# Spilling mix chunks from the used gate tile by another queue, and tying a weight's squares and parts to matmuls of the group before

## The chip, the core and the metric

The kernel runs on one core of a Trainium2 chip. A core has five engines that run their own instruction streams in order and meet only at semaphores: TensorE (matmul, "PE" in the profile, its weight loads "PEld"), VectorE ("DVE"), ScalarE ("ACT"), GpSimd ("POOL") and SyncE ("SP"), which here only issues DMAs. Matmuls write to PSUM, other operands lie in SBUF. The metric is the device time of one launch in microseconds; less is better.

## The reference

Two layers of a hybrid decoder, 512 tokens, model width 2048, float32. Cut to what matters:

```python
def _layer(x, ...):
    h = _rmsnorm(x, norm_g)
    proj = h @ w_in                       # 2048 x 7696
    (cv_h, cv_b, cv_c, cv_g, sb_q, sb_k, sb_v, sb_g,
     gl_q, gl_k, gl_v, gl_g, gl_lr) = jnp.split(proj, split_points, axis=-1)
    y_conv = _short_conv(cv_h, cv_b, cv_c, conv_w, conv_b) * silu(cv_g)
    y_sb = _stick_breaking(rms(sb_q), rms(sb_k), sb_v) * silu(sb_g)       # 8 heads of 128
    g = log_sigmoid(gl_lr @ gla_w_up + gla_b_up) / 16
    y_gla = _rmsnorm(_gla(gl_q, gl_k, gl_v, g), gla_on_g) * silu(gl_g)     # 4 heads, dk 64, dv 128
    mix = jnp.concatenate([y_conv, y_sb, y_gla], axis=-1)
    return x + mix @ w_out                # 2048 x 2048
```

`y_conv = B * conv3(C * h)` is a causal convolution of width 3. Stick-breaking attention weighs key j of query i by `sigmoid(z_ij)` times the product of `sigmoid(-z_ik)` over the keys k between them. `_gla` is gated linear attention with a decay per key channel. The gate of every branch is `silu` of its own projection.

## The kernel before

**Precision and groups.** Every large product is made of float16 parts: an operand is split into a high part and a low rest, and a product takes three matmuls (high by high, high by low, low by high). The weight columns of a layer are cut into 38 groups of 256 (30 of `w_in`, 8 of `w_out`; the list `specs`, lines 318 to 334), worked off one after the other. The order in a layer is: GLA v 0, v 1, q, k, gate 0, gate 1; conv h, c, g, b of half 0; then for j = 0 to 3 attention v, g, q, k; conv h, c, g, b of half 1; then the eight output groups. The text calls them "v 0", "g 0" (the gate of attention pair 0), "conv b" and so on.

**One weight's way.** `fetch(i)` (350) loads weight i as two halves of 1 MB into one of two staging buffers "st", from GpSimd's queue (SyncE's for the first three). `wmax` (366) has ScalarE square each half into a junk tile and add up, which gives two sums per partition; these are "the squares" (line 370). `wscale` (376) adds them over partitions on GpSimd (383) and makes a power of two of it on VectorE (386 to 400). `whi` and `wlo` (433, 442) write the parts: ScalarE the high part (436), VectorE the rest (444), a half at a time, into the pools "wh" and "wl" of three buffers each. When the last part is written the staging buffer is free, and the fetch of the weight after the next may start.

**Quick groups.** `QUICK_IN` and `QUICK` name groups (all attention g and k, conv h 1, some output groups) that are multiplied by a Strassen-like scheme with seven block products instead of eight (`project_quick`, 735; matmuls on lines 750 and 753). Their weight is split by `wsums` (462) into seven blocks, with sums of blocks between; one of these sums is made by an accumulating DMA from GpSimd (494). The parts take all three buffers of the pools and an extra pair, "w7". The sums of the activations that they need are made once per layer by `xsums` (727) for the input groups and `msums` (717) for the output groups.

**Where products land.** Three PSUM banks ("psp") serve all groups; each group takes two. In `project_quick` the accumulators pa and pd share one bank, pb and pf the other; pa and pd are copied or added to the output tile on lines 761 to 775, and a product into a bank waits for the copy that reads the same bank.

**Order of the work.** The order on each engine is not written by hand (except for the prologue, lines 107 to 645): a planner sets it when the kernel is built, from a priority (order in the program; `tc.high_priority` lifts it), readiness on a modelled clock, and free buffers. Tiles of one tag get their buffers in program order. `order(a, b)` (190) and `tc.issue_after` add an edge of issue order for the planner; they put no semaphore into the program. `weights()` (506) is called at the head of each group i: it fetches weight i + 2 and calls `load(i + 1)` (339, 449), which places squares, scale and parts of the next weight at high priority; the squares come behind `anchor[i]`, the first high part of weight i (the third or second of a quick one).

**The mix.** The outputs of the branches ("chunks" of 128 channels, 16 a layer) become two float16 parts in `mixsplit` (847): ScalarE the high one (857), VectorE the rest (858). Until the tile for all chunks exists, the parts of a chunk go into a "ga" buffer of the work pool, and SyncE spills them to DRAM (860, 256 KB each, 12 a layer); `mixload` (862) brings them back later. The work pool has two buffers per tag. "ga" is also the scratch tile of the gates in `project_gate` (802): for GLA and conv gates the chain is line 822 (copy out of PSUM), 824 to 826 and 828 on ScalarE, 827 and 829 on VectorE. The gates themselves lie in "g" tiles, two buffers: GLA gate 0, GLA gate 1, the conv gate, then g 0, g 1 and so on. A gate is last read where a branch output is multiplied by it: lines 1109 (GLA), 1161 (conv), 1247 (attention). Conv b's accumulators are read on line 1176, which needs the product of 1161.

**The tail of the GLA.** The loop at 999 handles two pairs of heads. At its end stand, per head, 1096 (VectorE), 1098 (ScalarE), 1100 (a matmul that averages squares), 1102 and 1103 (ScalarE), 1104 to 1109 (VectorE), then `mixsplit`. `conv_out` (1158) follows it in the program, then the attention loop (1254).

Of the kernel before, what the change touches and what calls it, by code (L numbers as in the profile page):

```python
# [17 lines left out]
P = 128  # L18
# [25 lines left out]
def hybrid_trunk(ctx, tc, x, norm_g, w_in, conv_w, conv_b, sb_qn_g, sb_kn_g,  # L44
# [294 lines left out]
    def load(i):  # L339
        with tc.high_priority():  # L340
            load_(i)

# [23 lines left out]
    def wmax(i, h):  # L366

        if h == 0:
            peak[i] = sm(2 + (i in narrow), "wm")
        S.activation(junk(HK * GW).rearrange("p (k n) -> p k n", k=HK), staged[i][h], AF.Square,  # L370
                     accum_out=peak[i][:, h:h + 1])
        if h and i in narrow:
            S.activation(junk(KT * LR).rearrange("p (k n) -> p k n", k=KT), narrow[i], AF.Square,
                         accum_out=peak[i][:, 2:3])

    def wscale(i):

        l, src, cols = specs[i]

        m = sm(1, "wq")  # L380
        if i:
            gm = sm(2 + (i in narrow), "wgm")
            G.partition_all_reduce(gm, peak.pop(i), P, RED.add)  # L383
            if i in narrow:
                V.tensor_tensor(gm[:, 0:1], gm[:, 0:1], gm[:, 2:3], ALU.add)
            V.tensor_tensor(m, gm[:, 0:1], gm[:, 1:2], ALU.add)
        else:

            ps = bank(psm, "m")[:, :1]
            pk = peak.pop(i)  # L390
            for j, (a, b) in enumerate(((ones, pk[:, 0:1]), (ones, pk[:, 1:2]), (pk[:, 2:3], pk[:, 2:3]))):
# [12 lines left out]

# [26 lines left out]
    anchor = {}  # L431

    def whi(i, h):
        wh = wpool.tile([P, HK, GX], F16, tag="wh", name=nm("wh"))
        wl = wpool.tile([P, HK, GX], F16, tag="wl", name=nm("wl"))
        hi = S.activation(wh[:, :, :GW], staged[i][h], AF.Copy, scale=scales[i])  # L436
        anchor.setdefault(i, hi)
# [23 lines left out]

    def wsums(i):
# [18 lines left out]
        if specs[i][1] is w_out:  # L481
# [6 lines left out]
            anchor[i] = split(b12, 2)  # L488
# [7 lines left out]
        anchor[i] = split(b22, 3)  # L496
# [9 lines left out]
    def weights():  # L506
# [3 lines left out]
        if i + 2 < len(specs):  # L510
            with tc.high_priority():
                fetch(i + 2)
        if i and i + 1 < len(specs):
            load(i + 1)
# [132 lines left out]
    for l in range(depth):  # L647
# [3 lines left out]
        def project_cols():  # L651
# [3 lines left out]
            for h in range(2):  # L655
                wh, wl = w[h]
                for c, o in enumerate(ps):
                    cs = slice(c * P, (c + 1) * P)
                    for kk in range(HK):
# [5 lines left out]
                        T.matmul(o, wl[:, kk, cs], xh[:, :, k, :], start=False, stop=en)  # L665
            return ps, u

        def tok_mm(o, ah, al, w, t, k, n, st_, en):
# [4 lines left out]
            T.matmul(o, al[:, t, k, :], wh[:, kk, :n], start=False, stop=en, skip_group_check=True)  # L673

        def project_toks(ah, al, late=()):
# [59 lines left out]
        def project_quick(src, sums, y, cols):  # L735
# [7 lines left out]
            def prod(o, w, a, start, stop=False):  # L743
                for t in range(1 if cols else 2):
                    for kk in range(HK):
                        for i, (p_, q_) in enumerate(((0, 0), (0, 1), (1, 0))):
                            st_ = start and t == kk == i == 0
                            en = stop and kk == HK - 1 and i == 2
                            if cols:
                                T.matmul(o, w[q_][:, kk, :], a[p_][:, :, kk, :], start=st_, stop=en,  # L750
                                         skip_group_check=True)
                            else:
                                T.matmul(o[:, t * P:(t + 1) * P], a[p_][:, t, kk, :], w[q_][:, kk, :], start=st_,  # L753
                                         stop=en, skip_group_check=True)
# [7 lines left out]
            prod(pb, wT2, s_, True)  # L762
# [26 lines left out]
        def project_by_token(ah, al, n):  # L789
# [3 lines left out]
            for t in range(NT):  # L793
                o = bank(psp, "p")
                for i, (a_, part) in enumerate(((ah, 0), (al, 0), (ah, 1))):
                    for k in range(KT):
                        T.matmul(o[:, :n], a_[:, t, k, :], w[k // HK][part][:, k % HK, :n],  # L797
                                 start=i == 0 and k == 0, stop=i == 2 and k == KT - 1)
# [48 lines left out]
        def mixsplit(k, y, s_):  # L847
# [6 lines left out]
            else:  # L854
                hl = wk([P, 2, NT, P], "ga", dt=F16)
# [3 lines left out]
            if not mix:  # L859
                nc.sync.dma_start(mixd[l][:, :, k, :], hl.rearrange("p i t c -> p (i t) c"))  # L860
# [74 lines left out]
        insums = xsums()  # L935
# [10 lines left out]
        for tag in ("qT", "kT"):  # L946
# [17 lines left out]
            qku.append(un)  # L964
        gq, gk = qk
# [33 lines left out]
        for p in range(2):  # L999
# [92 lines left out]
            for hh in range(2):  # L1092
# [17 lines left out]
                mixsplit(12 + 2 * p + hh, o_, gsc[p])  # L1110
# [47 lines left out]
        def conv_out(j, y, then=lambda: None):  # L1158
# [20 lines left out]
            for c in range(2):  # L1179
                mixsplit(2 * j + c, y[:, c, :], s_)  # L1180
# [10 lines left out]
        def attend(j, qT, kT, vh, vl, vu, g, s_):  # L1191
# [34 lines left out]
            def values(hh):  # L1226
# [23 lines left out]
                mixsplit(4 + 2 * j + hh, y.rearrange("p t c -> p (t c)"), s_)  # L1250
# [157 lines left out]
```

## Time and profile before

| | us |
|---|---|
| median of 3 runs | 1780.85 (1779.24 to 1786.48) |
| profiled execution | 1789.68 |
| its span | 1787.5 |
| TensorE busy | 1685.7 |
| VectorE busy | 1340.1 |
| ScalarE busy | 1131.2 |
| GpSimd busy | 218.2 |
| mean granted clock of TensorE | 0.981 |

The profile is of one execution. In its rows "L370" is line 370 of the kernel; "junk<-st" names the tiles written and read. A row of the timeline has start, duration, engine, line, operation, tiles and shape, and in brackets how long the engine stood idle just before it and what ended that. A row of the waits has who waited for whom: microseconds in total, times, the longest. Where several semaphores were waited for, the last one is named.

### The profile page before, as it was taken

How to read it: one execution, taken by the hardware profiler on the slowest of the kernel's cores; microseconds unless marked ns; L12 is line 12 of the kernel's file. 1: busy time of each engine (PE TensorE's matmuls, PEld its weight loads, DVE VectorE, ACT ScalarE, POOL GpSimd, SP SyncE). 2: the span in 40 equal slices, each digit the busy share in tenths (PEclk: the TensorE clock that was granted, in tenths of full speed). 3: DMA queues.
4: the chain of work that ended last, by engine and by line, in shares of the span. 5: the costliest groups of instructions: out<-in, count | busy, mean ns of one | idle time of the engine just before them, and what ended most of it. 6: DMA issues, size and time to landing. Idle time of an engine off the chain costs nothing.

```text
span 1787.5 us, 36869 instructions
## 1 busy us (share of the span) xinstructions
PE 1685.7 (94%) x15642; PEld 1306.6 (73%) x15642; DVE 1340.1 (75%) x2327; ACT 1131.2 (63%) x1619; POOL 218.2 (12%) x262
## 2 busy tenths in 40 slices
PE   7999995999999999999989999959999899999999
PEld 5644554888989884689976454649888888748898
DVE  8966887577777787686688577866777777768874
ACT  7667664576666676566665675556676666755652
POOL 1210110011111111011111101001111111100100
PEclk9999998999999999999999999989999999999999
DMA  7233341357656867355544233224576677763441
GB/s 241 92 98 95 95 118 55 76 131 136 143 136 143 143 166 206 77 163 169 192 98 142 90 100 106 60 59 111 110 170 103 138 134 165 223 150 102 158 144 49
DMA packets 204517, 227.25 MB, mean 127 GB/s; under 512 B 118770, under 2 KB 166204, under 8 KB 203840
## 3 DMA queue, kind: packets, MB, share of 16 engines
q0 software_dynamic: 58432, 162.54, 32.6%
q1 hardware_dynamic: 136912, 52.90, 14.4%
q10 hardware_dynamic: 9008, 9.45, 1.6%
q8 instruction: 122, 2.00, 0.5%
q14 instruction: 43, 0.35, 0.1%
HBM read 179.65 MB, written 14.68 MB: 109 GB/s over the span
## 4 chain that ended last, share of the span: by engine, by line
PE 19%; DVE 13%; DMA 12%; ACT 7%; issue 3%; POOL 1%; POOLq 0%; ACTq 0%; DVEq 0%
DMA st<-in_w_in_dram 5%; PE psp L753 5%; ACT junk L370 3%; DMA st<-in_w_out_dram 3%; PE psp L797 3%; DVE wl L477 3%; DMA qT<-qp 2%; PE psp L673 2%; PE psp L750 2%; PE psp L671 2%; PE psp L672 2%; PE psp L664 1%; PE psp L663 1%; PE psp L665 1%; DVE wl L444 1%
## 5 line engine op out<-in xcount | busy, mean ns | idle before, releaser
L370 ACT ACTIVATE junk<-st 128x2048 uint8<-128x2048 f32 x150 | 285.8, 1905 | 129.6 <-DMA st<-in_w_in_dram 94.9
L444 DVE SCALAR_TENSOR_TENSOR wl<-st,ws,wh 128x2048 f16<-128x2048 f32 x102 | 239.2, 2346 | 51.6 <-ACT wh L436 51.1
L671 PE MATMUL psp<-wh,m 128*128 128x256 f16 x960 | 261.8, 273 | 1.6 <-ACT m L1127 1.6
L672 PE MATMUL psp<-wl,m 128*128 128x256 f16 x960 | 261.8, 273 | 0.0
L673 PE MATMUL psp<-wh,m 128*128 128x256 f16 x960 | 261.8, 273 | 0.0
L436 ACT ACTIVATE wh<-st,ws 128x2048 f16<-128x2048 f32 x100 | 199.1, 1996 | 68.0 <-PE psp L664 32.2
L477 DVE SCALAR_TENSOR_TENSOR wl<-st,ws,wh 128x1024 f16<-128x1024 f32 x150 | 189.4, 1278 | 35.7 <-ACT wh L476 35.6
L476 ACT ACTIVATE wh<-st,ws 128x1024 f16<-128x1024 f32 x150 | 165.6, 1139 | 64.5 <-PE psp L673 33.6
L359 POOL DMA_DIRECT2D st<-in_w_in_dram x114 | 103.7, 926 | 476.9 <-DVE wl L444 219.8
L673 PE MATMUL psp<-wh,x 128*128 128x256 f16 x512 | 139.7, 273 | 0.0
L672 PE MATMUL psp<-wl,x 128*128 128x256 f16 x512 | 139.6, 273 | 0.0
L671 PE MATMUL psp<-wh,x 128*128 128x256 f16 x512 | 139.5, 273 | 0.0
L383 POOL PARTITION_ALL_REDUCE wgm<-wm x75 | 38.1, 508 | 811.1 <-ACT junk L370 797.7
L665 PE MATMUL psp<-x,wl 128*128 128x512 f16 x352 | 134.1, 381 | 2.2 <-DVE wl L444 2.2
L750 PE MATMUL psp<-s,wh 128*128 128x256 f16 x640 | 113.8, 279 | 23.6 <-ACT g L761 21.4
L663 PE MATMUL psp<-x,wh 128*128 128x512 f16 x352 | 134.2, 381 | 0.0
L664 PE MATMUL psp<-x,wh 128*128 128x512 f16 x352 | 133.9, 381 | 0.0
L663 PE MATMUL psp<-m,wh 128*128 128x512 f16 x352 | 133.4, 379 | 0.0
L664 PE MATMUL psp<-m,wh 128*128 128x512 f16 x352 | 133.4, 379 | 0.0
L665 PE MATMUL psp<-m,wl 128*128 128x512 f16 x352 | 133.2, 379 | 0.0
L665 PEld LDWEIGHTS <-wl 128*128 128x128 f16 x704 | 69.0, 98 | 83.2 <-DVE wl L444 2.7
L663 PEld LDWEIGHTS <-wh 128*128 128x128 f16 x704 | 69.0, 98 | 81.4 <-issue 1.7
(426 smaller groups left out, 4001.5 us busy)
## 6 DMA issues: line engine op xcount, KB each, us to landing
st<-in_w_in_dram POOLq DMA_DIRECT2D x114, 1024.0 KB, 8.3
st<-in_w_out_dram POOLq DMA_DIRECT2D x32, 1024.0 KB, 7.6
st<-st POOLq DMA_DIRECT2D x18, 512.0 KB, 9.5
st<-in_w_in_dram SPq DMA_DIRECT2D x6, 1024.0 KB, 11.8
mixd<-ga SPq DMA_DIRECT2D x24, 256.0 KB, 10.0
x<-in_x_dram SPq DMA_DIRECT2D x4, 1024.0 KB, 4.9
qT<-in_x_dram ACTq DMA_DIRECT2D x8, 512.0 KB, 4.7
qT<-xs ACTq DMA_DIRECT2D x8, 512.0 KB, 4.1
```

What stands on the lines that cost most here:

```text
L370: S.activation(junk(HK * GW).rearrange("p (k n) -> p k n", k=HK), staged[i][h], AF.Square, accum_out=peak[i][:, h:h + 1])
L436: hi = S.activation(wh[:, :, :GW], staged[i][h], AF.Copy, scale=scales[i])
L444: V.scalar_tensor_tensor(wl[:, :, :GW], staged[i][h], scales[i], wh[:, :, :GW], ALU.mult, ALU.subtract)
L476: hi = S.activation(h_, b, AF.Copy, scale=sc)
L477: V.scalar_tensor_tensor(l_, b, sc, h_, ALU.mult, ALU.subtract)
L663: T.matmul(o, wh[:, kk, cs], xh[:, :, k, :], start=st_, stop=False)
L664: T.matmul(o, wh[:, kk, cs], xl[:, :, k, :], start=False, stop=False)
L665: T.matmul(o, wl[:, kk, cs], xh[:, :, k, :], start=False, stop=en)
L671: T.matmul(o, ah[:, t, k, :], wh[:, kk, :n], start=st_, stop=False, skip_group_check=True)
L672: T.matmul(o, ah[:, t, k, :], wl[:, kk, :n], start=False, stop=False, skip_group_check=True)
L673: T.matmul(o, al[:, t, k, :], wh[:, kk, :n], start=False, stop=en, skip_group_check=True)
L750: T.matmul(o, w[q_][:, kk, :], a[p_][:, :, kk, :], start=st_, stop=en, skip_group_check=True)
```

## The change

Three parts.

1. `mixsplit` gets the gate tile of its chunk as `dead`. The two float16 parts are written over it, in place of a "ga" tile, and GpSimd's queue issues the spill, in place of SyncE's. The gate tile is then free when the spill has landed.
2. `load` and the anchors go. `weights()` leaves two functions in `hooks`: the squares of weight i + 1, and its scale and parts. The projections of group i call the first behind their first product of three matmuls, and the second behind a later one: after a quarter of the group in the plain forms (24 of 96 matmuls by columns; two of four token tiles of the first half; the first of four token tiles), after the second of seven products in the quick one. The first square and the first VectorE step of the scale get an `order` edge to that matmul; the rest follows from them by data, or by high priority alone.
3. `insums = xsums()` is traced behind the GLA q and k projections, not ahead of them.

```diff
@@ wmax / wscale
-        S.activation(junk(HK * GW)..., staged[i][h], AF.Square, accum_out=peak[i][:, h:h + 1])
+        sq = S.activation(junk(HK * GW)..., staged[i][h], AF.Square, accum_out=peak[i][:, h:h + 1])
...
+        return sq
...
-            V.tensor_tensor(m, gm[:, 0:1], gm[:, 1:2], ALU.add)
+            first = V.tensor_tensor(m, gm[:, 0:1], gm[:, 1:2], ALU.add)
...
+        return first
@@ load
-    def load(i):
-        with tc.high_priority():
-            load_(i)
-    def load_(i):
-        with tc.issue_after(anchor[i - 1].ins):
-            for h in range(2):
-                wmax(i, h)
-        wscale(i)
-        if i in quick:
-            wsums(i)
-            return
-        for h in range(2):
-            whi(i, h)
-            wlo(i, h)
+    hooks = []
+    def squares(i, mm):
+        with tc.high_priority():
+            for h in range(2):
+                a = wmax(i, h)
+                if not h:
+                    order(a, mm)
+    def parts_of(i, mm):
+        with tc.high_priority():
+            order(wscale(i), mm)
+            if i in quick:
+                wsums(i)
+                return
+            for h in range(2):
+                whi(i, h)
+                wlo(i, h)
+    def hook(mm):
+        if hooks:
+            hooks.pop(0)(mm)
@@ weights
-            load(i + 1)
+            hooks.extend([lambda mm: squares(i + 1, mm), lambda mm: parts_of(i + 1, mm)])
@@ project_cols
-                        T.matmul(o, wl[:, kk, cs], xh[:, :, k, :], start=False, stop=en)
+                        mm = T.matmul(o, wl[:, kk, cs], xh[:, :, k, :], start=False, stop=en)
+                        if not h and not c and kk in (0, HK - 1):
+                            hook(mm)
@@ project_toks
-                        tok_mm(o, ah, al, w, t, k, GW, k == 0 and t % 2 == 0, k == lastk)
+                        mm = tok_mm(o, ah, al, w, t, k, GW, k == 0 and t % 2 == 0, k == lastk)
+                        if not t and k == 0 or t == 1 and k == rounds[0][-1]:
+                            hook(mm)
@@ project_quick
+                            if start and t == kk == 0 and i == 2 and o is pa:
+                                hook(mm)
+                return mm
...
-            prod(pb, wT2, s_, True)
+            hook(prod(pb, wT2, s_, True))
@@ project_by_token
+                        if not t and (not i and not k or i == 2 and k == KT - 1):
+                            hook(mm)
@@ mixsplit
-        def mixsplit(k, y, s_):
+        def mixsplit(k, y, s_, dead):
...
-                hl = wk([P, 2, NT, P], "ga", dt=F16)
+                hl = dead.bitcast(F16).rearrange("p (i t c) -> p i t c", i=2, t=NT)
...
-                nc.sync.dma_start(mixd[l][:, :, k, :], hl.rearrange("p i t c -> p (i t) c"))
+                nc.gpsimd.dma_start(mixd[l][:, :, k, :], hl.rearrange("p i t c -> p (i t) c"))
@@ callers
-        insums = xsums()
         scr = ...
...
+        insums = xsums()
         gq, gk = qk
...
-                mixsplit(12 + 2 * p + hh, o_, gsc[p])
+                mixsplit(12 + 2 * p + hh, o_, gsc[p], gg[p][:, hh, :])
...
-                mixsplit(2 * j + c, y[:, c, :], s_)
+                mixsplit(2 * j + c, y[:, c, :], s_, g[:, c, :])
...
-                mixsplit(4 + 2 * j + hh, y.rearrange("p t c -> p (t c)"), s_)
+                mixsplit(4 + 2 * j + hh, y.rearrange("p t c -> p (t c)"), s_, g[:, hh, :])
```

More of the change, by code (lines that the diff above doesn't have):

```diff
@@ L369, in wmax @@
             peak[i] = sm(2 + (i in narrow), "wm")
-        S.activation(junk(HK * GW).rearrange("p (k n) -> p k n", k=HK), staged[i][h], AF.Square,
-                     accum_out=peak[i][:, h:h + 1])
+        sq = S.activation(junk(HK * GW).rearrange("p (k n) -> p k n", k=HK), staged[i][h], AF.Square,
+                          accum_out=peak[i][:, h:h + 1])
         if h and i in narrow:
@@ L390, in wscale @@
             pk = peak.pop(i)
+            first = None
             for j, (a, b) in enumerate(((ones, pk[:, 0:1]), (ones, pk[:, 1:2]), (pk[:, 2:3], pk[:, 2:3]))):
@@ L512, in weights @@
                 fetch(i + 2)
+        assert not hooks
         if i and i + 1 < len(specs):
-            load(i + 1)
+            hooks.extend([lambda mm: squares(i + 1, mm), lambda mm: parts_of(i + 1, mm)])
         return loaded.pop(i)
@@ L672, in tok_mm @@
             T.matmul(o, ah[:, t, k, :], wl[:, kk, :n], start=False, stop=False, skip_group_check=True)
-            T.matmul(o, al[:, t, k, :], wh[:, kk, :n], start=False, stop=en, skip_group_check=True)
+            return T.matmul(o, al[:, t, k, :], wh[:, kk, :n], start=False, stop=en, skip_group_check=True)
         def project_toks(ah, al, late=()):
@@ L796, in project_by_token @@
                     for k in range(KT):
-                        T.matmul(o[:, :n], a_[:, t, k, :], w[k // HK][part][:, k % HK, :n],
-                                 start=i == 0 and k == 0, stop=i == 2 and k == KT - 1)
+                        mm = T.matmul(o[:, :n], a_[:, t, k, :], w[k // HK][part][:, k % HK, :n],
+                                      start=i == 0 and k == 0, stop=i == 2 and k == KT - 1)
+                        if not t and (not i and not k or i == 2 and k == KT - 1):
+                            hook(mm)
                 ps.append(o)
```

14 lines of the change are left out of this document (6 added, 8 removed).

## The prediction

> **What bounds the kernel now.** I read the page's head, then TensorE's waits, then the timelines of ScalarE and VectorE around the longest of them.
>
> ```profile
> span 1787.5 us, 36869 instructions
> PE 1685.7 (94%) x15642; PEld 1306.6 (73%) x15642; DVE 1340.1 (75%) x2327; ACT 1131.2 (63%) x1619; POOL 218.2 (12%) x262
> ```
>
> TensorE bounds it: 1685.7 of 1787.5 us are busy, so 101.8 us of idle time is all that a change of order can win, and the rest is matmuls that the change leaves alone. The waits of TensorE (total, times, longest, us):
>
> ```profile
> PE psp L750 <- ACT g L761: 21.4, 2, 10.8
> PE psp L750 <- ACT g L768: 14.4, 8, 3.1
> PE psm L1100 <- ACT e L1098: 14.2, 2, 7.1
> ...
> PE psp L753 <- DVE wl L477: 4.2, 6, 1.4
> PE psp L753 <- ACT kT L768: 4.2, 2, 3.0
> ```
>
> Two causes hold most of it. The first stands once per layer, at the end of the gated linear attention (21.4 + 14.2 = 35.6 us). ScalarE in layer 0:
>
> ```profile
> 286.25 1.90 ACT L370 ACTIVATE junk<-st 128x2048 uint8<-128x2048 f32 x1
> ...
> 288.71 1.90 ACT L370 ACTIVATE junk<-st 128x2048 uint8<-128x2048 f32 x1
> ...
> 291.12 4.25 ACT L476 ACTIVATE wh<-st,ws 128x1024 f16<-128x1024 f32 x4
> 295.28 0.57 ACT L1263 ACTIVATE v<-psp 128x512 f16<-128x512 f32 x1
> 297.66 0.63 ACT L1098 ACTIVATE e<-za 128x512 f32<-128x512 f32 x1 [1.80 <-DVE e L1107]
> ...
> 313.64 0.63 ACT L824 ACTIVATE ga<-g 128x512 f32<-128x512 f32 x1 [5.06 <-DMA mixd<-ga]
> 314.18 0.36 ACT L761 ACTIVATE g<-psp 128x256 f32<-128x256 f32 x1
> ```
>
> L824 is the conv gate's, whose projection was copied out long before (L822 below). It waits for a "ga" buffer, and the last GLA chunk holds that until its spill has landed at 313.6. L761, which TensorE needs, stands behind it on ScalarE. VectorE shows what else hangs on it:
>
> ```profile
> 298.74 0.68 DVE L1264 SCALAR_TENSOR_TENSOR v<-psp,v 128x512 f16<-128x512 f32 x1
> ...
> 308.61 0.75 DVE L858 SCALAR_TENSOR_TENSOR ga<-za,gsmix,ga 128x512 f16<-128x512 f32 x1 [0.79 <-ACT ga L857]
> ...
> 321.96 1.23 DVE L1161 TENSOR_TENSOR kT<-kT,g 128x1024 f32<-128x1024 f32 x1
> 323.22 1.41 DVE L1176 SCALAR_TENSOR_TENSOR kT<-psp,wu,kT 128x512 f32<-128x512 f32 x2
> ...
> 327.44 1.41 DVE L858 SCALAR_TENSOR_TENSOR ga<-kT,csmix,ga 128x512 f16<-128x512 f32 x2 [0.79 <-ACT ga L857]
> ```
>
> L1176 frees the two accumulators of conv b. Until 324.6 these hold two of the three "psp" banks, so "v 0" and "g 0" share one, and "g 0" cannot begin before L1264 at 299.4. That is why TensorE has nothing else to run in the 7.1 us before L1100.
>
> The second cause is ScalarE standing at a square whose weight hasn't landed:
>
> ```profile
> 417.87 1.91 ACT L370 ACTIVATE junk<-st 128x2048 uint8<-128x2048 f32 x1 [4.11 <-DMA st<-in_w_in_dram]
> ...
> 419.78 0.36 ACT L768 ACTIVATE g<-psp 128x256 f32<-128x256 f32 x1
> ...
> 420.19 0.27 PE L750 MATMUL psp<-x,w7h 128*128 128x256 f16 x1 [2.04 <-ACT g L768]
> 420.30 0.27 PE L750 MATMUL psp<-x,w7l 128*128 128x256 f16 x1
> ```
>
> L768 (a copy out of PSUM) is queued behind it, and TensorE's last product behind L768. (Matmuls follow each other at 0.11 us here, so a product of 24 takes 2.7.) Over the kernel ScalarE stands so for 94.9 us at the input weights alone:
>
> ```profile
> ACT junk L370 <- DMA st<-in_w_in_dram: 94.9, 43, 5.5
> ```
>
> **The change part by part.** *Spill out of the gate tile (T1).* The "ga" buffer of a spill goes, so L824 waits for nothing and the conv gate can run when its copies are done, 70 us earlier.
>
> ```profile
> 259.35 0.38 PE L665 MATMUL psp<-x,wl 128*128 128x512 f16 x1
> ```
>
> Conv b then leaves its banks soon after its last matmul at 259.7, and its spill's parts are done 6.9 us later (L1161 to the end of the last L858 above), at about 267, and "v 0" and "g 0" have three banks. What takes the place of "ga" is the "g" tile: "g 0" is the fourth gate of the layer on two buffers, and may begin when conv's gate tile or the second GLA gate's is free, now after landing of their spills.
>
> ```profile
> 240.83 0.67 ACT L822 ACTIVATE g<-psp,wu 128x512 f32<-128x512 f32 x1
> ...
> 236.55 0.74 DVE L858 SCALAR_TENSOR_TENSOR ga<-za,gsmix,ga 128x512 f16<-128x512 f32 x1
> ...
> L359 POOL DMA_DIRECT2D st<-in_w_in_dram x114: 882/899/1592, 59.0 to 1546.6; - x114
> ...
> DMA to landing us min/median/max: 5.5/8.3/19.0
> ...
> DMA to landing us min/median/max: 3.4/10.0/11.6
> ```
>
> The last two are GpSimd's weight fetches and SyncE's spills. A spill from GpSimd isn't in the trace; its landing lies between 3.4 and 19.0 us, and I take 10, nearest to the spills' own median. Conv's gate is then free at 267 + 0.9 + 10 = 278, at the worst 287; "g 0" asks for it at about 291 (L1098 ends at 298.3, 7.1 us after "v 0"). So the bound above: both waits go, 7.1 + 10.8 us, with the slow clock after them:
>
> ```profile
> L750 PE MATMUL psp<-s,wh x16: 273/418/418, 314.6 to 319.2; 128*128 128x256 f16 x16
> ...
> 260.00:285.00 25.00, 23.10 (x247) 20.27 (x245) 19.25 (x40) 12.16 (x30) 0.00 (x0) 1.00 0.01 2
> ...
> 285.00:335.00 50.00, 30.46 (x227) 23.79 (x225) 32.84 (x47) 28.19 (x37) 2.18 (x3) 0.83 0.22 64
> ```
>
> (columns: PE, PEld, DVE, ACT, POOL busy, clock, DMA share, GB/s.) The granted clock is 0.83 there; 24 matmuls started over 4.6 us, not 2.6. Together 20 us a layer. The bound below: if "g 0" gets the GLA gate's tile, it waits for that spill: 309.4 + 0.9 + 3.4 to 19.0 = 313.7 to 329.3, against 314.2 now: from 0.5 us won to 15 us lost. Between them stands VectorE: 19.25 + 32.84 = 52.1 us of work in these 75 us. Twenty less leave 55 us, 95% full. I take 14 a layer (61 us, 85%): **-28**.
>
> *Squares and parts behind matmuls (T2).* The squares (two of 1.9 us) move from the end of the group before to the first matmuls of the current one, when their data have lain there for most of a group. That takes ScalarE's stall out of the way of L768: 14.4 + 4.2 = 18.6 us at most, 0 at least. In a quick group (seven products of 2.7 us) the new places are at 0.3 to 4.3 us, while L761 is due by 5.4; the parts begin at 5.4, when the first buffer of the pool is free anyway, and L768 is due between 13.5 and 16.2. I take **-13**; some of the eight waits are other casts' doing.
>
> *Later parts (T5).* Now squares, reduce and first casts cannot be ready before the group begins.
>
> ```profile
> L383 POOL PARTITION_ALL_REDUCE wgm<-wm x75: 350/400/1660, 40.7 to 1743.4; - x75
> ...
> st<-st POOLq DMA_DIRECT2D x18, 512.0 KB, 9.5
> ...
> L477 DVE SCALAR_TENSOR_TENSOR wl<-st,ws,wh 128x1024 f16<-128x1024 f32 x150 | 189.4, 1278 | 35.7 <-ACT wh L476 35.6
> ```
>
> For a quick weight the accumulating DMA follows the reduce: issued 4.9 us into the group, landed at 14.4, and with an add and two casts of some 1.3 us each the second block is ready by 19; its product is due at the group's end, 21 (192 matmuls at 0.11), and 2.7. Some 5 us of slack, against 0.7 to 1.4 for the waits on L477 now. From 0 to 10, I take **+2**.
>
> *Conv gate's own slot (T3).* L822 now waits for the first GLA gate's spill: its L858 ends 237.3, so landed at 241.6 to 257.2, by 10 at 248.2. Conv b has a third bank and needs a second after 24 of its 96 matmuls, at some 243.5. But the tail before it loses two squares, 3.8 us, as the one at 286 does. 0 to 14 a layer; near 248.2 less 3.8 I take **+1** each.
>
> *At nothing.* 24 issues of 0.9 us on GpSimd, covered by its 88% idle time; if they stood ahead of a reduce, 0.9 us each. SyncE loses them, and its transposes stand behind fewer waits. The sums of the first quick group move behind the q and k projections:
>
> ```profile
> L691 DVE TENSOR_TENSOR s<-zw,s x12: 1207/1212/1219, 48.9 to 970.4; 128x1024 f16<-128x1024 f32 x12
> ```
>
> They are first read by "g 0" at 300, 200 us later; the cover gone, 24 such steps of 1.2 us would be 29 us of VectorE beside the GLA. In attention a gate's spill has time:
>
> ```profile
> 469.43 0.72 ACT L857 ACTIVATE ga<-e,bsmix 128x512 f16<-128x512 f32 x1 [1.29 <-DVE e L1247]
> ...
> 493.32 0.40 ACT L761 ACTIVATE g<-psp 128x256 f32<-128x256 f32 x1
> ```
>
> 23 us less 1.5 for L858, 0.9 and 10 leave 11.
>
> The Trainium skill ("SBUF — State Buffer", section "SBUF: two separate sides") speaks against GpSimd's queue: GpSimd writes these descriptors itself and is locked out while VectorE holds their shared port; a DMA of 620 ns is said to take 3100 beside such an operation. Here 114 issues took 882 to 1592 ns with VectorE 75% busy, so the trace shows no such lock; by the rule, as an estimate, 2.5 us for each of some eight gate slots would make the sum 20 us worse.
>
> **Sum**, against the profiled execution's 1789.68 us (span 1787.5): -28 - 13 + 2 + 2 = -37, so 1752.7. The median of the runs, 1780.85, is 8.8 lower; there the same 37 give 1744.
>
> **The rivals.**
> (a) *Only the stalls go.* "g 0" gets the GLA gate's tile, landed at 309.4 + 0.9 + 10 = 320.3, 6.1 us after L761 now. The first wait goes: 2 × (6.1 - 7.1) - 13 + 4 = -11, 1770. For it: that tile is the older of the two. Against: conv's would be free by 287.
> (b) *The order is not what it says.* The new edges are issue order without a semaphore, placed by the planner's clock, not the chip's; squares may still meet late data. T2 and T5 go: 1780.9 - 28 + 2 = 1755.
> (c) *VectorE or the weight chain takes over.* At 75% busy on the mean, the gaps reappear at casts: T1 and T2 halve and T5 goes to 10: -20 + 12 = -8, 1773 to 1785, no clear change.
> (d) *Slower: GpSimd's queue holds the spill.* One in-order queue now has fetches, reduces and spills. As (a), but the second GLA gate's spill stands behind a fetch that waits for VectorE:
>
> ```profile
> POOL st L359 <- DVE w7l L477: 187.1, 14, 19.7
> ```
>
> That is 187.1/14 = 13.4 us more for "g 0", and for all that ScalarE has behind L761: 2 × (6.1 + 13.4 - 7.1) - 13 + 4 = +16, 1797. It is slower from a queue wait of 5.5 us on; in attention, with 11 us in hand, only from 11. For it: such a fetch follows the parts of the quick "g 0", due just then. Against: the planner puts the spill where its data are due, and conv's tile may spare the wait.
>
> The Trainium skill ("DMA: Bandwidth & Descriptors", "Two DMAs through the same engine are not ordered") adds that descriptors within one queue start in order, so a spill issued after a fetch also starts after it. No run here shows that yet; by the fetches' median it would cost 8.3 us there, 17 for both layers and 1787 in (a)'s place.
>
> **How the numbers follow.** The forecast has 0.50, (a) 0.16, (b) 0.10, (c) 0.09, (d) 0.15. A measurement of this kernel tells 0.5%, 8.9 us, from no change: faster 0.50 + 0.16 + 0.10 = 0.76, same 0.09, slower 0.15. The range begins at 1710, with both terms near their bounds (40 + 19 is 1722, and 12 for the small waits of TensorE that I didn't cost), and ends at 1786, within (c); (d) and the tails are left out.
>
> **What would show it.** Right: "ACT g L761" and "ACT e L1098" nearly gone from TensorE's waits; L824 of the conv gate some 70 us earlier; L370's waits on the DMA gone; clock 1.00 where 0.83 stands. Wrong: a wait on a "mixd" landing before L761 or L822; more TensorE waits on L477 or L444; GpSimd's spills standing ahead of L383. The prediction fails if VectorE's casts come late in every group, or if the planner's new order opens gaps that no row of before shows.

## The result and the profile after

The changed kernel takes **1713.6 us** (median of 3 runs, 1712.7 to 1717.4) against 1780.85: a ratio of 0.962, 95% interval 0.958 to 0.966. That is 67 us less, where the forecast had 37 (1744); the range began at 1710, so it only just holds the result. The profiled execution took 1717.44 us, and its page begins:

```profile
span 1715.7 us, 36876 instructions
PE 1669.4 (97%) x15642; PEld 1297.0 (76%) x15642; DVE 1331.3 (78%) x2327; ACT 1129.4 (66%) x1619; POOL 239.7 (14%) x286
```

Beside the page of before this splits the 71.8 us of span in two. TensorE's idle time fell from 101.8 to 46.3 us (55.5), and the same 15642 matmuls took 16.3 us less of busy time. The second part goes with TensorE's granted clock, whose mean rose from 0.981 to 0.992. An estimate from windows of 0.5 us (TensorE's busy time times what the clock lacks to 1.00) puts the time lost to a slow clock at 23.1 us before and 10.4 after, 12.7 of the 16.3 us; the rest stays open. The prediction's sentence that idle time "is all that a change of order can win" was wrong by this part; of the clock it counted 2 us a layer.

(In the new file L366 is the square, L841 and L843 the gate's copy and first step, L778, L782 and L785 the three evictions of a quick group, L877 and L879 the spill's second part and its DMA. Before, these were L370, L822 and L824, L761, L765 and L768, L1098, L858 and L860.)

TensorE's longest waits after, in total, times, longest:

```profile
PE psz L1222 <- DMA kT<-qp: 10.9, 2, 6.4
PE psp L764 <- ACT g L785: 6.0, 6, 1.7
...
PE psm L1259 <- DVE e L1266: 2.5, 2, 1.8
```

The two waits of the linear attention's end (21.4 and 14.2 us before) aren't in the list any more, and the one on the third eviction is down from 14.4 to 6.0. The first row is new: score matmuls that wait for transposed keys. The stretches of before, by windows (columns as in the prediction):

```profile
260.00:285.00 25.00, 25.00 (x249) 21.91 (x247) 24.69 (x53) 17.12 (x38) 3.73 (x4) 1.00 0.44 103
285.00:335.00 50.00, 49.98 (x521) 44.58 (x520) 41.09 (x63) 38.31 (x56) 9.45 (x10) 1.00 0.38 106
```

TensorE runs through, 521 matmuls where there were 227, at a clock of 1.00 where it was 0.83. VectorE is busy for 24.69 of 25 us and then 41.09 of 50, and TensorE doesn't wait for it. ScalarE in the same layer:

```profile
239.30 1.27 ACT L841 ACTIVATE g<-psp,wu 128x512 f32<-128x512 f32 x2 [0.82 <-DMA mixd<-g]
242.35 1.14 ACT L843 ACTIVATE ga<-g 128x512 f32<-128x512 f32 x2
...
291.25 0.39 ACT L778 ACTIVATE g<-psp 128x256 f32<-128x256 f32 x1
```

The conv gate's L843 runs at 242, 71 us earlier than before. Its copy now waits for a spill of the linear attention's first gate (the bracket), but only 0.82 us, and TensorE waits for none of it.

What is left of the wait on the third eviction is seen at the end of "g 1" (timeline of the changed kernel; first GpSimd, then ScalarE, then TensorE):

```profile
381.86 1.81 POOL L355 DMA_DIRECT2D st<-in_w_in_dram  x2 [7.62 <-DVE w7l L486]
```

```profile
389.02 1.91 ACT L366 ACTIVATE junk<-st 128x2048 uint8<-128x2048 f32 x1 [4.88 <-DMA st<-in_w_in_dram]
...
390.93 0.36 ACT L785 ACTIVATE g<-psp 128x256 f32<-128x256 f32 x1
```

```profile
387.17 0.27 PE L683 MATMUL psp<-wh,x 128*128 128x256 f16 x1
...
391.34 0.27 PE L764 MATMUL psp<-x,w7h 128*128 128x256 f16 x1 [1.39 <-ACT g L785]
```

The fetch could start only when the quick weight's last cast had freed the staging buffer; its first half landed at 389.0. The square of that weight hangs on the first matmul of the next group (L683), which TensorE runs at 387.2, before the last product of "g 1". So a square still stands at its data with L785 behind it, for 1.4 us instead of 2. One sign of the prediction, the squares' waits on the DMA "gone", came true by a little over half: they fell from 94.9 to 41.6 us.

```profile
ACT junk L366 <- DMA st<-in_w_in_dram: 41.6, 18, 5.2
```

### The profile page after: what moved, and what is told of

Read it like the earlier page. It is cut to its first block, busy times and chain, and to the rows that moved or that the text cites. A ratio compares the mean times of both kernels' runs of the same rounds, so it can differ in the third digit from the quotient of the medians.

```text
span 1715.7 us, 36876 instructions
## 1 busy us (share of the span) xinstructions
PE 1669.4 (97%) x15642; PEld 1297.0 (76%) x15642; DVE 1331.3 (78%) x2327; ACT 1129.4 (66%) x1619; POOL 239.7 (14%) x286
## 3 DMA queue, kind: packets, MB, share of 16 engines
q1 hardware_dynamic: 111952, 46.61, 14.2%
## 4 chain that ended last, share of the span: by engine, by line
PE 75%; DVE 10%; DMA 7%; ACT 4%; issue 2%; POOL 0%; DVEq 0%; ACTq 0%; POOLq 0%
PE psp L767 13%; PE psp L675 8%; PE psp L674 8%; PE psp L673 8%; PE psp L684 8%; PE psp L685 8%; PE psp L683 8%; PE psp L814 6%; PE psp L764 3%; DMA st<-in_w_in_dram 3%; DVE wl L486 2%; DMA kT<-qp 2%; ACT junk L366 2%; DMA th<-za 1%; PE psz L1014 1%
## 5 line engine op out<-in xcount | busy, mean ns | idle before, releaser
L366 ACT ACTIVATE junk<-st 128x2048 uint8<-128x2048 f32 x150 | 285.1, 1901 | 42.8 <-DMA st<-in_w_in_dram 41.6
L683 PE MATMUL psp<-wh,m 128*128 128x256 f16 x960 | 261.7, 273 | 0.0
L683 PE MATMUL psp<-wh,x 128*128 128x256 f16 x512 | 139.6, 273 | 0.0
L673 PEld LDWEIGHTS <-wh 128*128 128x128 f16 x704 | 69.3, 98 | 81.8 <-issue 3.6
L674 PEld LDWEIGHTS <-wh 128*128 128x128 f16 x704 | 69.5, 99 | 81.5 <-issue 3.5
```

The costliest lines, as they stand in the source:

```text
L366: sq = S.activation(junk(HK * GW).rearrange("p (k n) -> p k n", k=HK), staged[i][h], AF.Square, accum_out=peak[i][:, h:h + 1])
L673: T.matmul(o, wh[:, kk, cs], xh[:, :, k, :], start=st_, stop=False)
L674: T.matmul(o, wh[:, kk, cs], xl[:, :, k, :], start=False, stop=False)
L683: T.matmul(o, ah[:, t, k, :], wh[:, kk, :n], start=st_, stop=False, skip_group_check=True)
```

## The experiments

The ratios are of mean times, to the kernel before, which ran beside each of them. Span, PE busy and "idle" (span less TensorE's busy time) are of one profiled execution each. The busy time varies between executions: e6 has nearly the waits of before and 5.9 us less of it. So differences of a few us in span say less than the ratios.

| kernel | ratio to before (95%) | span | PE busy | idle |
|---|---|---|---|---|
| before | 1 | 1787.5 | 1685.7 | 101.8 |
| changed | 0.962 (0.958 to 0.966) | 1715.7 | 1669.4 | 46.3 |
| e1 gate tile, SyncE's queue | 0.972 (0.968 to 0.976) | 1731.2 | 1672.3 | 58.9 |
| e2 gate tile, GpSimd's queue | 0.972 (0.968 to 0.975) | 1730.0 | 1675.1 | 54.9 |
| e3 hooks alone | 0.986 (0.982 to 0.990) | 1764.8 | 1684.0 | 80.8 |
| e4 changed, SyncE's queue | 0.964 (0.960 to 0.969) | 1713.1 | 1669.8 | 43.3 |
| e5 gate tile, linear attention alone | 0.973 (0.970 to 0.975) | 1731.1 | 1671.7 | 59.4 |
| e6 gate tile, the others alone | 1.001 (0.999 to 1.004) | 1781.4 | 1679.8 | 101.6 |
| e7 changed, parts with the squares | 0.964 (0.961 to 0.966) | 1717.5 | 1669.8 | 47.7 |
| e8 changed, keys before loads | 0.958 (0.955 to 0.961) | 1710.2 | 1670.2 | 40.0 |
| e9 changed, squares and parts 5 us later | 0.982 (0.979 to 0.985) | 1751.9 | 1679.0 | 72.9 |
| e10 e8 and e9 together | 0.967 (0.965 to 0.969) | 1728.5 | 1671.0 | 57.5 |
| e11 changed, sums at the old place | 0.962 (0.960 to 0.964) | 1719.1 | 1669.4 | 49.7 |
| e12 e8, squares alone 2.6 us later | 0.976 (0.972 to 0.980) | 1733.2 | 1676.1 | 57.1 |

**The spill alone, by either queue (e1, e2).** Edits to the kernel before (the calls pass the gate tile, as in the change):

```diff
-                hl = wk([P, 2, NT, P], "ga", dt=F16)
+                hl = dead.bitcast(F16).rearrange("p (i t c) -> p i t c", i=2, t=NT)
```

and, in e2 alone:

```diff
-                nc.sync.dma_start(mixd[l][:, :, k, :], hl.rearrange("p i t c -> p (i t) c"))
+                nc.gpsimd.dma_start(mixd[l][:, :, k, :], hl.rearrange("p i t c -> p (i t) c"))
```

> The kernel before with one edit: the split mix chunk goes into the gate tile that it has just used up, and is still sent by SyncE's queue; squares and parts stay where they were. Theory A (the 'ga' buffer held until the spill landed is what stopped TensorE at the end of the linear attention, and the slow clock after it is part of its price): the waits before the output normaliser's matmuls and before the first product of 'g 0' go in both layers, 2 x (7.1 + 10.8) = 36 us of idle time and some 14 us of slow clock, so about 1725 to 1735 against 1781; the waits on the third eviction of a quick group (14.4 us) stay. Rival B ('g 0' then waits for the tile of a linear-attention gate until that has landed): only the first wait goes, 1765 to 1772. Rival C (the squares standing between the evictions at the end of the linear attention were the cause): 1775 to 1785, both waits stay.

> As the run with SyncE's queue, but the 24 spills are issued by GpSimd. Theory A (the queue is worth nothing): within 4 us of the run with SyncE's queue. Rival D (in GpSimd's queue a spill stands behind fetches and holds the gate tile longer): slower than that run by 10 us or more. Rival E (GpSimd's spills land some 2 to 3 us sooner, and SyncE's transposes no longer stand behind them): faster by 5 to 10 us.

Both came out at 0.972. Theory A holds and B and C fall: the squares are where they were, and the waits at the end of the linear attention go all the same (from 21.4 and 14.2 us to 1.9 and 1.6). The longest wait of e1:

```profile
PE psp L750 <- ACT g L768: 14.5, 6, 3.1
```

The span falls by 56.3 us: 42.9 of idle time and 13.4 of busy time (by the ratio some 50 us). The wait on L768 stays at 14.5, as it should with the squares in their old place. GpSimd's queue is worth nothing either way, so D and E fall.

**Which of the spills (e5, e6).** The gate tile for the chunks from 12 on (the linear attention's) or for those below 12:

```diff
-                hl = wk([P, 2, NT, P], "ga", dt=F16)
+                hl = (dead.bitcast(F16).rearrange("p (i t c) -> p i t c", i=2, t=NT) if k >= 12
+                      else wk([P, 2, NT, P], "ga", dt=F16))
```

> The kernel before with the spills of the linear attention's four chunks alone put into their gate tiles (SyncE's queue); those of the convolution and of the attention keep 'ga'. Theory A (the linear attention's last chunks hold the 'ga' that the conv gate needs): the whole gain of the run with all spills moved (56 us of span), 1730 to 1740. Rival G (the convolution's or the attention's own 'ga' spills held something too): 1745 to 1770, with waits left at the end of the linear attention or in the attention.

> The other way round: the convolution's and the attention's spills go into gate tiles, the linear attention's four chunks keep 'ga'. Theory A: nothing, 1778 to 1790, both waits at the end of the linear attention stay (14 and 21 us). Rival G: 1730 to 1765.

0.973 and 1.001: the eight spills of the linear attention (four a layer) carry all of it, the other sixteen nothing. In e6 both waits stand as before:

```profile
PE psp L750 <- ACT g L761: 19.1, 2, 9.9
PE psm L1101 <- ACT e L1099: 14.2, 2, 7.1
```

**The hooks alone (e3).** The changed kernel with the old "ga" tile, SyncE's queue and the sums at their old place:

```diff
-                hl = dead.bitcast(F16).rearrange("p (i t c) -> p i t c", i=2, t=NT)
+                hl = wk([P, 2, NT, P], "ga", dt=F16)
...
-                nc.gpsimd.dma_start(mixd[l][:, :, k, :], hl.rearrange("p i t c -> p (i t) c"))
+                nc.sync.dma_start(mixd[l][:, :, k, :], hl.rearrange("p i t c -> p (i t) c"))
```

> The other half alone: squares, reduce and parts behind matmuls of the current group, as in the changed kernel; the spill keeps its own 'ga' buffer and SyncE's queue, and the sums of the first quick group are at their old place. Theory A: ScalarE's waits on the fetches fall as in the changed kernel (from 95 us to about 42), the waits on the third eviction go down from 14.4 us to 5 or less, and the waits at the end of the linear attention (14.2 and 21.4 us) stay: 1765 to 1772. Rival C (the squares were the cause there too): these go as well, 1715 to 1735. Rival F (the order edges move nothing): 1779 to 1785.

0.986, some 25 us where I expected 12: no theory had it whole. Its waits:

```profile
PE psp L764 <- DVE v L1283: 8.7, 2, 4.4
PE psp L764 <- ACT g L778: 8.7, 2, 4.4
...
PE psp L764 <- ACT g L785: 8.5, 8, 2.0
```

The third eviction's wait went from 14.4 to 8.5. The rest is at the end of the linear attention. The conv gate's L843 is still late there, though 9 us earlier than before, and the stalls of 7.1 and 10.8 us a layer became two of 4.4. L843 waits for no landing any more; it stands in ScalarE's queue behind the last chunk's L876, which waits for VectorE:

```profile
304.31 0.72 ACT L876 ACTIVATE ga<-za,gsmix 128x512 f16<-128x512 f32 x1 [3.34 <-DVE za L1128]
304.94 0.61 ACT L843 ACTIVATE ga<-g 128x512 f32<-128x512 f32 x1
```

That "ga" puts it there follows from the changed kernel: it differs from e3 by the tile, the queue and the place of the sums, of which the last two are worth nothing (e4 and e11 below), and has L843 at 242.

So the halves overlap: 56.3 (e1) and 22.7 (e3) of span are 79.0, and the change has 71.8 (by the ratios 51, 25 and 68). Behind e1 the hooks are worth 15.5.

**The queue, the sums and the moment of the parts, taken out of the changed kernel (e4, e11, e7).**

```diff
 e4
-                nc.gpsimd.dma_start(mixd[l][:, :, k, :], hl.rearrange("p i t c -> p (i t) c"))
+                nc.sync.dma_start(mixd[l][:, :, k, :], hl.rearrange("p i t c -> p (i t) c"))
 e11
+        insums = xsums()
         scr = [wk([P, 2, 2, seq], *a, F16) for a in (("qp", 1), ("th", 2), ("th", 2))]
...
-        insums = xsums()
         gq, gk = qk
 e7
-            hooks.extend([lambda mm: squares(i + 1, mm), lambda mm: parts_of(i + 1, mm)])
+            hooks.append(lambda mm: (squares(i + 1, mm), parts_of(i + 1, mm)))
```

> The changed kernel with one edit undone: the spills are issued by SyncE. Theory A (the queue is worth nothing): 1710 to 1719, as the changed kernel (1714). Rival E (SyncE's queue was the better part of the gain): 1725 or more, with waits of the gate or of the key transposes behind spills. If the two new waits of the score matmuls on the key transposes (6.4 and 4.5 us) come from the queue, they change here: with SyncE sending both they would be longer.

> The changed kernel with the sums of the first quick group (24 steps of 1.2 us on VectorE) back ahead of the linear attention. Theory A (the move is worth nothing, since VectorE is 75% busy and the sums are read 200 us later): 1710 to 1720. Rival Q (they crowd VectorE in the linear attention's first part, and the move is part of the gain): 1722 or more, with waits on VectorE between 130 and 230 us.

> The changed kernel, but the reduce and the parts of the next weight hang on the same first matmul as its squares instead of a later one (the first quick product's end, the first round's end). Theory A (the later parts cost 2 us in all, at most 10): 1704 to 1718. Rival H (holding the parts back is itself a gain, since early parts stand between the copies out of PSUM): 1722 or more, and the waits on the third eviction grow above 6 us.

0.964, 0.962 and 0.964: each within the interval of the changed kernel, so none of the three is worth what can be measured here, and E, H and Q fall. The waits for the keys, which I expected to be longer in e4 with SyncE sending both, were shorter (7.7 us against 10.9). How long a spill is under way differs, though; from GpSimd in the changed kernel, then from SyncE in e4:

```profile
L879 POOL DMA_DIRECT2D mixd<-g x24: 851/907/1615, 224.0 to 1469.8; - x24
...
  ACT g L841: 2.2, 2
...
DMA to landing us min/median/max: 3.1/7.6/10.9
```

```profile
L879 SPq DMA_DIRECT2D mixd<-g x24: 512/513/617, 223.8 to 1469.7; - x24
...
DMA to landing us min/median/max: 2.8/5.3/11.5
```

GpSimd takes 907 ns to issue one where SyncE takes 513, and the data land 2.3 us later at the median. Only the conv gate's copies wait for them, 2.2 us in two places (the middle row), and no less from SyncE's queue.

**The new wait on the keys (e8).** In the changed kernel SyncE sends, around the first of the two waits (the second column is the time of a row's instructions in SyncE's queue):

```profile
618.28 7.50 SPq L887 DMA_DIRECT2D m<-mixd  x4
626.61 13.23 SPq L1337 DMA_TRANSPOSE kT<-qp  x2
```

GpSimd had sent a weight fetch just before:

```profile
625.09 1.76 POOL L355 DMA_DIRECT2D st<-in_w_in_dram  x2 [5.12 <-DVE wl L442]
```

The two transposes take 13.2 us, with that fetch and four loads under way. e8 orders the loads behind the keys:

```diff
-                    nc.sync.dma_start(mix[i][:, :, ks, :], mixd[l][:, i * NT:(i + 1) * NT, ks, :])
+                    order(nc.sync.dma_start(mix[i][:, :, ks, :], mixd[l][:, i * NT:(i + 1) * NT, ks, :]), keys[-1])
...
-                    nc.sync.dma_start_transpose(nT_[:, i].rearrange("p t h c -> p (t h) c"), parts[:, i])
+                    keys.append(nc.sync.dma_start_transpose(nT_[:, i].rearrange("p t h c -> p (t h) c"), parts[:, i]))
```

> The changed kernel, with the loads of the spilled chunks ordered behind the last key transposes in SyncE's queue. In the changed kernel two loads of 0.75 MB and two smaller stand ahead of them, and TensorE waits 6.4 and 4.5 us for the transposed keys. Theory K (it is this order): these two waits go, 1701 to 1708. Rival L (the transposes are slow because the weight fetches fill the DMA engines at the same time): the waits stay at 3 us or more each, 1709 to 1716. Rival M (the loads then come too late for the out projection): a new wait on m, 1714 or more.

In e8, on SyncE (the loads follow at 633) and in TensorE's waits:

```profile
627.12 6.00 SPq L1337 DMA_TRANSPOSE kT<-qp  x2
```

```profile
PE psz L1222 <- DMA kT<-qp: 6.3, 2, 3.2
```

The transposes take 6.0 us instead of 13.2, though the same fetch goes out at 625.7, and the waits fall from 10.9 to 6.3: K for somewhat less than half of it. The rest is L's number (3 us each) but not L's cause: with the loads gone from their path the transposes aren't slow beside the fetch. They start late, since VectorE splits the keys only at 627. The ratio, 0.958, is the best of all; its interval (0.955 to 0.961) overlaps the changed kernel's, so that it is faster than that isn't shown.

**Squares and parts later still (e9, e10, e12).** In a group that follows a quick one, e9 hangs squares and parts together on the end of the second token tile's first round; e10 is e8 with this.

```diff
-            hooks.extend([lambda mm: squares(i + 1, mm), lambda mm: parts_of(i + 1, mm)])
+            if i - 1 in quick and i not in quick:
+                hooks.extend([lambda mm: None, lambda mm: (squares(i + 1, mm), parts_of(i + 1, mm))])
+            else:
+                hooks.extend([lambda mm: squares(i + 1, mm), lambda mm: parts_of(i + 1, mm)])
```

e12 is e8 with the squares alone later, on the end of the first token tile's first round:

```diff
+            first = rounds[0][-1] if cursor[0] - 2 in quick and specs[cursor[0] - 1][1] is w_in else 0
...
-                        if not t and k == 0 or t == 1 and k == rounds[0][-1]:
+                        if not t and k == first or t == 1 and k == rounds[0][-1]:
```

> The changed kernel, except that in a group which follows a quick one the squares and the parts of the next weight hang together on the end of the second token tile's first round (some 5 us later). Theory N (what is left of the third eviction's wait, 6.0 us in six places, comes from a square that still stands ahead of it in ScalarE's queue, since its fetch could start only when the quick weight's last cast had freed the staging buffer, some 7 us before): these waits go, ScalarE's wait on the fetches falls from 42 us to under 15, 1705 to 1712. Rival P (the parts are then late, the quick weight after it most of all): new waits of TensorE on casts, 1714 to 1730.

> Both edits at once on the changed kernel: loads of the spilled chunks behind the key transposes, and the later squares after a quick group. If N and K hold and add, 1698 to 1706; if the later parts cost as much as the waits they take away (P), 1708 to 1716.

> The changed kernel with the loads of the spilled chunks behind the key transposes (as in the earlier run of that alone, 1711), and in a group after a quick one the squares alone 2.6 us later, on the end of the first token tile's first round; the parts stay where the change put them. Theory N (a square ahead of the third eviction makes what is left of that wait, 6.5 us): it goes, ScalarE's wait on the fetches falls below 20 us, 1701 to 1707. Rival P (even 2.6 us make the reduce and the parts behind it late, as 5 us did): new waits on the values' and the key projections' inputs, 1714 or more.

All three came out on the side of P, e9 and e10 further than P said: 0.982, 0.967 and 0.976, so some 35 us worse than the changed kernel for e9, 17 worse than e8 for e10 and 32 worse than e8 for e12. The loss doesn't grow with the delay: e10's squares are later than e12's, and it lost less. In the profiled executions both stand idle for 57 us. The wait on L785 did go, as N has it. e12 on ScalarE:

```profile
384.60 0.38 ACT L786 ACTIVATE g<-psp 128x256 f32<-128x256 f32 x1 [1.38 <-PE psp L765]
391.72 1.01 ACT L1231 ACTIVATE za<-psz,nzun 128x896 f32<-128x896 f32 x1 [6.73 <-DMA th<-za]
...
394.44 1.92 ACT L366 ACTIVATE junk<-st 128x2048 uint8<-128x2048 f32 x1
```

The third eviction (L786 there) now goes before the square. But the square, 2.6 us later by its hook, has come to stand behind the scores' sigmoids (L1231), which wait themselves, and starts at 394.4, 5.6 us after e8's on ScalarE:

```profile
388.81 1.91 ACT L366 ACTIVATE junk<-st 128x2048 uint8<-128x2048 f32 x1 [4.81 <-DMA st<-in_w_in_dram]
```

The reduce on GpSimd follows, in e8 and then in e12:

```profile
394.32 0.40 POOL L380 PARTITION_ALL_REDUCE wgm<-wm  x1 [4.71 <-ACT junk L366]
```

```profile
400.57 0.40 POOL L380 PARTITION_ALL_REDUCE wgm<-wm  x1 [11.72 <-ACT junk L366]
```

Behind the reduce GpSimd issues the accumulating DMA of the next quick weight. In e12 VectorE comes to the sum that it makes (L506) before it has landed, and stands there; what follows in its queue is late by that, the copy of the attention's values out of PSUM (L1267) too:

```profile
DVE st L506 <- DMA st<-st: 19.7, 6, 3.9
```

```profile
409.75 1.23 DVE L506 TENSOR_TENSOR st<-st 128x1024 f32<-128x1024 f32 x1 [3.90 <-DMA st<-st]
...
419.82 0.87 DVE L1267 SCALAR_TENSOR_TENSOR e<-psm,vu,g 128x256 f32<-128x256 f32 x2
```

TensorE waits for L1267 as often and as long in e12, and for the same copy in e9 (the last two rows):

```profile
PE psm L1260 <- DVE e L1267: 20.3, 6, 4.0
```

```profile
PE psz L1225 <- DMA kT<-qp: 22.5, 2, 13.3
PE psm L1262 <- DVE e L1269: 19.6, 6, 4.0
```

(In the changed kernel L1259 waits 2.5 us for L1266.) VectorE's wait at this DMA is 24.2 us in e9 and 24.6 in e10; the changed kernel and e8 have none. e9's long wait for the keys (22.5 us) is down to 1.6 in e10, by e8's edit. What the 1.4 us at the third eviction buy is an early start of the reduce, and of the DMA behind it.

## Why the prediction was right, and where its sizes were off

**T1, the spill (-28): right in mechanism, half of its size.** e1 measured 56 us of span in the profiled execution, and some 50 by the ratio. The cause as the prediction put it is shown from both sides: the spills of the linear attention give all of it (e5), the others none (e6). One reading was off: L824 waits not for the last chunk's spill but for the one before it, issued at 303.8 and landed at 313.6, shortly after a weight fetch had gone out from GpSimd's queue (first the fetch, then that spill and who waited for it):

```profile
303.43 1.78 POOL L359 DMA_DIRECT2D st<-in_w_in_dram  x2 [12.16 <-DVE w7l L477]
```

```profile
L860 SPq DMA_DIRECT2D mixd<-ga x1: 513/513/513, 303.8 to 303.8; - x1
...
  ACT ga L824: 5.1, 1
```

Two terms were mis-sized.
- "Together 20 us a layer" is what e1 shows at the place itself: the two waits went from 35.6 to 3.5 us, and the time lost to the slow clock there (estimated as above) from 7.9 to 0, which is 40 in two layers. The clock's part of it was too small, since it had been read from one of two slow stretches (windows of the kernel before, clock in the third column from the right). The other 16 us of e1 lie elsewhere and had no term: TensorE's waits on copies into "kT" tiles in later quick groups fell from 10.9 to 1.0 us, and some 6 us more of slow clock went, which vary from one execution to the next (outside the linear attention's end it is 15.2 us in before and 6.6 in e6).

```profile
295.00:300.00 5.00, 1.66 (x2) 0.65 (x3) 5.00 (x6) 1.49 (x3) 0.00 (x0) 0.50 0.00 0
...
310.00:315.00 5.00, 0.41 (x3) 0.28 (x3) 0.00 (x0) 1.36 (x3) 0.00 (x0) 0.50 0.77 238
315.00:320.00 5.00, 4.47 (x23) 3.06 (x22) 1.54 (x3) 3.39 (x7) 0.00 (x0) 0.61 0.00 0
```

- "I take 14 a layer (61 us, 85%)" then took 6 off for VectorE. Nothing of that came: in the changed kernel VectorE is 99% busy from 260 to 285, with TensorE running through. A full engine isn't a late one, as long as what TensorE waits for stands at the front of its queue.

That 1713.6 lies within the range is owed to the 12 us allowed there for waits that weren't costed: both terms at their bounds gave 1722.

**T2, the squares (-13), with T5 (+2).** Behind e1 the hooks gave 15.5 us of span against the 11 of these two terms, but not in the places named. Of the 14.5 us at the third eviction 8.5 went. Smaller waits on evictions and casts, which I left out of the sum and allowed 12 us for in the range, went too, and the keys' new wait took back 10.9 us (the last sentence of the prediction, new gaps that no row of before shows, came true for these). What failed inside T2 is "their data have lain there for most of a group": it isn't so after a quick group, where the fetch lands 1.8 us after the hooked matmul starts. T5 at its place is nothing (e7). Its slack of "some 5 us" was near: in e8 the accumulating DMA goes out at 394.96, and with the 8.5 us that e12's took it would land at 403.5, an estimate, 4.3 us before VectorE takes the sum. But squares that are 2.6 us later by their hook made the reduce 6.3 us late in e12, which is more than that, and cost about 30 us.

**T3 (+1 each)** is 2.2 us on ScalarE for both layers and nothing on TensorE. **The terms at nothing** were nothing: issues on GpSimd (e2, e4), sums (e11).

**The rivals.** (a) falls: "g 0" waits for no tile, in e1 either. (b) falls as a whole, since the hooks do gain; a part of it lives in the square that still meets late data. (c) falls: VectorE is fuller and TensorE waits less. (d) falls: e1 and e2 agree, and e4 agrees with the changed kernel.

The two sentences on the Trainium skill end the same way. The lock of "SBUF — State Buffer", section "SBUF: two separate sides", isn't seen: 24 spills were issued in 851 to 1615 ns beside a VectorE that is 78% busy, and the 20 us by that rule didn't come. (The page ties the lock to certain operations of VectorE; whether this kernel's are such, no run here shows.) For the order of starts ("DMA: Bandwidth & Descriptors", "Two DMAs through the same engine are not ordered") no run here shows a cost: all spills from GpSimd's queue landed within 10.9 us.

Open: why the planner's new order puts the keys' split as late as 627 (the part of that wait which e8 left), why the waits on copies into "kT" go with the spills, and whether a place for the squares exists that keeps the reduce early and lets the third eviction pass. No run here tells.

## What to carry to other kernels

When a helper takes its temporary from a ring that others use too, look for who asks for that ring next and what is queued behind him: here eight DMAs that held a tile until they had landed (10.0 us at the median) cost 50 to 56 us. Count a stall of TensorE with the slow clock after it, once for each stall (2 us here), and don't take a discount for an engine only because it is nearly full. Before moving an early step out of the way of a small wait, see what it would then stand behind and which DMA hangs on it: 1.4 us saved at an eviction cost up to 4.0 at the values.

## What the runs showed of the hardware

After which gaps TensorE's clock falls. The length of a gap alone doesn't decide it. The same gap of 1.70 us, at the same place, lost the clock in the profiled execution of before and kept it in that of the changed kernel (TensorE's row behind the gap and the window around it, first before, then changed):

```profile
38.92 0.42 PE L551 MATMUL psz<-ident,x 128*128 128x128 f32 x1 [1.70 <-DVE x L560]
```

```profile
38.00:43.00 5.00, 4.08 (x22) 3.59 (x23) 4.64 (x7) 3.55 (x6) 0.86 (x1) 0.66 0.01 3
```

```profile
38.79 0.44 PE L561 MATMUL psz<-ident,x 128*128 128x128 f32 x2 [1.70 <-DVE x L570]
```

```profile
38.00:43.00 5.00, 4.21 (x39) 3.94 (x39) 4.65 (x7) 4.37 (x6) 0.86 (x1) 1.00 0.02 3
```

Before, the gap of 2.04 us at 420.2, which the prediction shows, lost it too, while one of 3.15 us at 1392 kept it at 1.00:

```profile
421.00:425.00 4.00, 4.00 (x24) 2.88 (x22) 0.59 (x4) 2.36 (x3) 1.59 (x2) 0.57 1.37 97
```

In the traces of before, e1 and the changed kernel 13 of 25 gaps of 1.70 to 3.15 us were followed by a slow stretch, and all those of 4.46 us and more. A slow stretch holds some 3 to 6.5 us of work at 0.50, and costs half of that. A longer stall didn't cost more: before, two of 7.1 and 10.8 us a layer lost 7.9 us to the clock in two layers (estimated as above), and in e3 two of 4.4 us lost 8.4.

The Trainium skill ("TensorE: Matmul & The Clock Gate", section "What's actually happening") puts the bound at an idle window of about 3.4 us and the way back at as much sustained work. The traces here differ in the first: half of the gaps that were shorter than this lost the clock. For the way back they show 3 to 6.5 us.
